# A delta-rule recurrence kept per head: 64x64 state blocks on the quadrants of TensorE

## The chip, the cores and the metric

The kernel runs on one core of one Trainium2 chip. The time is the device time of one execution in microseconds (us); "before" is the median of three runs. A profile of one execution on the same chip goes with it. The engines are named as in the profile: PE is TensorE (matmuls; PEld its weight loads), DVE is VectorE, ACT is ScalarE, POOL is GpSimd, SP is SyncE, which here issues most of the DMAs.

## The reference, cut to what matters

One layer of a hybrid decoder: an input projection, three groups of heads (sparse attention, a recurrence, a memory attention), and an output projection. It is done for a prompt of 1,024 positions and for eight single-position samples. The part that is changed is the recurrence of the prompt, four heads of 64, in float32:

```python
def step(s, inp):
    r_t, k_t, v_t, w_t, kk_t, b_t = inp
    sa = jnp.einsum('bhvk,bhk->bhv', s, -kk_t)
    s = s * w_t[:, :, None, :] + sa[..., None] * b_t[:, :, None, :] + v_t[..., None] * k_t[:, :, None, :]
    return s, jnp.einsum('bhvk,bhk->bhv', s, r_t)
s_fin, ys = lax.scan(step, s0.astype(jnp.float32), xs)
```

Each head has a state of 64x64. The final states are an output of their own.

## The kernel before

**The phases.** Phase 1 projects the prompt through the 28 column blocks of the input weights (`p_pr`: three float32r products for each of eight slices of 128, for the two halves H of the prompt) and runs the recurrence beside it. At its end it makes the keys for attention (`attn_keys`, `prompt_cmp`) and the memory keys (`mem_kv`). Phase 2 is the prompt's attention, phase 3 the samples and the output projection.

**The recurrence in chunks.** The prompt is cut into four quarters Q of 256 positions and each quarter into four chunks n of 64 (n = 2t + p). `rwkv_prep(Q)` makes the inputs, and `rwkv_state(Q)` makes, for each chunk and head, a 64x64 triangular inverse in half-steps of tiny products (`p_iy`, `p_it`), then `p_x`, then four things that the change is about:
- `p_g`: from `W` and the transposed inputs `bkT` and `AM` the transition `PT` of the state (plus the identity, added on DVE) and the read-out `GT`.
- `p_z`: for each chunk the new state, as `bkT x UV` plus `PT x Z`, summed in PSUM; DVE scales it by the decay `gC` and makes `Zn`, which is `Z` of the next chunk. This is the only part that runs one chunk after the other.
- `p_yy`: the output of two chunks, as `GT x Z` plus `AM x UV`.
- `y_c`, the copy of the output by ACT, and `rwkv_out`, its normalisation.

Two heads lie together in one 128x128 state `Z[:, c]`. Only its two diagonal 64x64 blocks hold states; the products fill the off-diagonal blocks too, and `self.blockm` zeroes them when `Zn` is made (L970).

**What sets the order.** `drive(work, fill)` draws the recurrence's steps with priority (`AHEAD`). Each `yield n` of a step is a length in us; `drive` multiplies it by `SLACK` (1.3) and draws that much of the column blocks (`fill`: the first `EARLY` = 17 of the list `cols`) behind it. Before the second quarter's `rwkv_state` stands

```python
while self.open:
    next(fill)
```

which finishes the column block that is open. The remaining blocks, `late`, four of them, come after the fourth quarter, in turn with the making of keys (`bg`). A list scheduler then sets each engine's order by its own estimates, so late blocks can be put between the recurrence's last steps. TensorE's instructions of the fill go through a helper: their line is L87 up to the end of `drive` and for the recurrence, L307 for the late blocks. The pool `pw` holds three PSUM banks, which all tiles of the recurrence share.

Of the kernel before, what the change touches and what calls it, by code (L numbers as in the profile page):

```python
# [114 lines left out]
class Step:  # L115
# [566 lines left out]
    def rwkv_open(self):  # L682
        tc, nc, I = self.tc, self.nc, self.I
        c = self.rc
        cm = self.c_rw = c.tile([128, 480], F32, name="c_rw")
        nc.scalar.dma_start(cm[:], I["c_rw"])
        self.maskA = cm[:, 0:128]
        self.blockm = cm[:, 128:256]
# [23 lines left out]
        self.Z = c.tile([128, 2, 128], F32, name="Z0", tag="Z", bufs=3)  # L712
# [116 lines left out]
    def rwkv_state(self, Q):  # L829
# [103 lines left out]
        GT, PT = [None] * 2, [None] * 2  # L933
        for t in range(2):
# [3 lines left out]
            half = [slice(p * 64, p * 64 + 64) for p in range(2)]  # L938
            for c in range(2):
                for pg, o, p in zip(pgs, half, range(2)):  # L940
                    PE.matmul(pg[:, c * 128:(c + 1) * 128], W[t][o, 2 * c:2 * c + 2, :].rearrange("p a b -> p (a b)"),
                              bkT[t][o, c, p, :], start=True, stop=True)
            for h in range(4):
                for pg, o, p in zip(pgs, half, range(2)):
                    PE.matmul(pg[half[h % 2], 256 + (h // 2) * 64:320 + (h // 2) * 64], W[t][o, h, :],
                              AM[o, 2 * p + t, h, 64:128], start=True, stop=True)
            for p, pg in enumerate(pgs):
                V.tensor_tensor(PT[t][:, :, p, :], pg[:, 0:256].rearrange("p (c e) -> p c e", c=2),
                                bc(I[:, None, :], [128, 2, 128]), op=OP.add)
            for p, pg in enumerate(pgs):  # L950
                V.tensor_tensor(GT[t][:, :, p, :], pg[:, 256:384].rearrange("p (c e) -> p c e", c=2),
                                ar[:, :, t, 1, p, :], op=OP.add)
            yield 1.1
        ys = []
        for t in range(2):
            pyy = self.pw.tile([128, 4, 64], F32, name="p_yy", tag="w")
            Zs = []
            for p in range(2):
                n = 2 * t + p
                Z = self.Z  # L960
                Zs.append(Z)
                pz = self.pw.tile([128, 2, 128], F32, name="p_z", tag="w")
                Zn = self.rc.tile([128, 2, 128], F32, name="Zn", tag="Z", bufs=3)
                for c in range(2):
                    PE.matmul(pz[:, c, :], bkT[t][:, c, p, :], UV[:, n, 2 * c:2 * c + 2, :].rearrange("p a b -> p (a b)"),
                              start=(c == 0), stop=False, skip_group_check=True)
                for c in range(2):
                    PE.matmul(pz[:, c, :], PT[t][:, c, p, :], Z[:, c, :], start=False, stop=(c == 1), skip_group_check=True)
                for c in range(2):
                    V.scalar_tensor_tensor(Zn[:, c, :], pz[:, c, :], self.gC[:, c, n:n + 1], self.blockm,  # L970
                                           op0=OP.mult, op1=OP.mult)
                self.Z = Zn
                if p == 0:
                    yield 0.8
            half = [slice(64 - p * 64, 128 - p * 64) for p in range(2)]
            for c in range(2):
                for p, o in enumerate(half):
                    PE.matmul(pyy[o, 2 * c:2 * c + 2, :].rearrange("p a b -> p (a b)"), GT[t][:, c, p, :], Zs[p][:, c, :],
                              start=(c == 0), stop=False, skip_group_check=True)
            for h in range(4):  # L980
                for p, o in enumerate(half):
                    PE.matmul(pyy[o, h, :], AM[:, 2 * p + t, h, 64:128], UV[:, 2 * t + p, h, :], start=False, stop=(h == 3),
                              skip_group_check=True)
# [29 lines left out]
    def rwkv_close(self):  # L1013
        nc, O = self.nc, self.O
        ps = self.pw.tile([128, 2, 128], F32, name="p_s", tag="w")
        for c in range(2):
            nc.tensor.transpose(ps[:, c, :], self.Z[:, c, :], self.ident[:])
        S = self.rs.tile([128, 2, 128], F32, name="S_out", tag="W0")
        nc.scalar.activation(S[:], ps[:], AF.Copy)
        for h in range(4):  # L1020
            o = slice((h % 2) * 64, (h % 2) * 64 + 64)
            nc.sync.dma_start(O["wkv_prompt"][0, 0, h], S[o, h // 2, o])

# [1377 lines left out]
def host_consts():  # L2401
# [10 lines left out]
    rw = np.zeros((128, 480), np.float32)  # L2412
# [8 lines left out]
    rw[:, 448:480] = s == c  # L2421
    for h in range(2):
# [54 lines left out]
```

## Time and profile before

| what | value |
|---|---|
| median of three runs | 948.95 us (948.5 to 950.33) |
| the profiled execution | 948.73 us, its span 946.9 us |
| PE busy | 911.0 us, 96% of the span |
| DVE busy | 656.6 us, 69% |
| ACT busy | 436.5 us, 46% |
| recurrence, first `p_am` to last `p_yy` | about 93 to 420 us of the span |
| key making and late blocks | about 427 to 500 us |

A matmul's record lasts some 0.2 to 0.4 us from its first row to its last result, and several overlap. So how long a stretch of matmuls occupies PE is read from one start to the next, not from the durations. Each float32 product of the program stands as two instructions in the trace; a float32r product is one.

### The profile page before, as it was taken

How to read it: one execution, taken by the hardware profiler on the slowest of the kernel's cores; microseconds unless marked ns; L12 is line 12 of the kernel's file. 1: busy time of each engine (PE TensorE's matmuls, PEld its weight loads, DVE VectorE, ACT ScalarE, POOL GpSimd, SP SyncE). 2: the span in 40 equal slices, each digit the busy share in tenths (PEclk: the TensorE clock that was granted, in tenths of full speed). 3: DMA queues.
4: the chain of work that ended last, by engine and by line, in shares of the span. 5: the costliest groups of instructions: out<-in, count | busy, mean ns of one | idle time of the engine just before them, and what ended most of it. 6: DMA issues, size and time to landing. Idle time of an engine off the chain costs nothing.

```text
span 946.9 us, 24305 instructions
## 1 busy us (share of the span) xinstructions
PE 911.0 (96%) x9655; PEld 776.5 (82%) x9655; DVE 656.6 (69%) x2029; ACT 436.5 (46%) x979; POOL 179.5 (19%) x270
## 2 busy tenths in 40 slices
PE   8999999999999999999997999999999998999998
PEld 8998888778897888768885888888888887887976
DVE  7668689847693786984447776756678996548454
ACT  7564324233432243213435666566576765324211
POOL 2000000000000000000103444344355675112010
PEclk9999999999999999999999999999999999999999
DMA  8521323131331118216337425140210035976661
GB/s 277 133 68 35 102 58 101 45 81 50 96 94 44 42 61 195 61 57 169 119 101 206 155 69 177 53 143 25 70 41 9 9 113 157 328 248 216 184 233 47
DMA packets 134985, 105.91 MB, mean 112 GB/s; under 512 B 34673, under 2 KB 121272, under 8 KB 134744
## 3 DMA queue, kind: packets, MB, share of 16 engines
q1 hardware_dynamic: 129880, 92.64, 33.4%
q0 software_dynamic: 3200, 10.49, 3.1%
q8 instruction: 76, 1.25, 0.5%
q10 hardware_dynamic: 1792, 1.23, 0.4%
q14 instruction: 37, 0.30, 0.1%
HBM read 85.74 MB, written 22.78 MB: 115 GB/s over the span
## 4 chain that ended last, share of the span: by engine, by line
PE 71%; DVE 16%; ACT 6%; DMA 3%; issue 2%; POOL 1%; SPq 0%; DVEq 0%; ACTq 0%; POOLq 0%
PE p_pr L87 20%; PE p_out L87 9%; PE p_pr L307 7%; PE p_s L87 5%; PE p_pT L87 4%; PE p_o L87 4%; PE p_hid L87 3%; ACT p L1402 3%; DVE p L1401 2%; PE p_z L87 2%; PE p_sc L87 1%; PE p_it L87 1%; PE p_tk L87 1%; DVE pt L1374 1%; PE p_q L87 1%
## 5 line engine op out<-in xcount | busy, mean ns | idle before, releaser
L87 PE MATMUL p_pr<-h,whi 128*128 128x512 f32 (+2 forms) x976 | 238.2, 337 | 0.0
L87 PEld LDWEIGHTS p_pr<-h,whi 128*128 128x128 f32 x976 | 158.7, 190 | 16.9 <-issue 2.6
L87 PE MATMUL p_pr<-h,wlo 128*128 128x512 f32 (+2 forms) x488 | 158.0, 327 | 0.6 <-DVE wlo L284 0.6
L1427 POOL TENSOR_SCALAR p<-p,fac,gates 128x640 f32<-128x640 f32 (+7 forms) x128 | 104.2, 826 | 106.2 <-DVE fac L1424 60.6
L1402 ACT ACTIVATE p<-p,nm 128x640 f32<-128x640 f32 (+7 forms) x128 | 93.0, 728 | 53.1 <-DVE nm L1401 46.6
L87 PEld LDWEIGHTS p_pr<-h,wlo 128*128 128x128 f32 x488 | 92.0, 190 | 9.1 <-DVE wlo L284 0.8
L87 PE MATMUL p_pT<-ident,p 128*128 128x128 f32 x528 | 70.9, 279 | 5.1 <-ACT pt L1372 1.6
L1076 POOL MEMSET w2d<- 128x128 f32 x1 | 0.2, 205 | 398.1 <-PE p_yy L87 398.1
L1401 DVE CUSTOM_DVE_ANT_0 p<-p_s,bmask 128x512 f32<-128x512 f32 (+7 forms) x96 | 60.3, 662 | 18.6 <-PE p_s L87 15.1
L87 PEld LDWEIGHTS p_pT<-ident,p 128*128 128x128 f32 x528 | 57.0, 141 | 16.0 <-issue 6.6
L307 PE MATMUL p_pr<-h,whi 128*128 128x264 f32 (+2 forms) x320 | 68.8, 310 | 0.4 <-ACT whi L283 0.4
L87 PE MATMUL p_o<-pt,vs 128*64 128x128 f32 x1056 | 67.9, 276 | 0.4 <-DVE cat L1460 0.4
L87 PE MATMUL p_s<-kh,qs 128*128 128x512 f32 (+3 forms) x191 | 65.9, 357 | 1.3 <-DVE nm L1401 1.3
L87 PEld LDWEIGHTS p_o<-pt,vs 128*64 128x64 f32 x1056 | 57.0, 137 | 7.2 <-issue 3.8
L283 ACT ACTIVATE whi<-wraw 128x1024 fp32r<-128x1024 f32 x34 | 36.0, 1058 | 57.8 <-PE p_pr L87 47.6
L284 DVE TENSOR_TENSOR wlo<-wraw,whi 128x1024 fp32r<-128x1024 f32 x33 | 40.3, 1222 | 31.4 <-ACT whi L283 31.4
L87 PE MATMUL p_s<-kl,qs 128*128 128x512 f32 (+3 forms) x192 | 60.6, 336 | 0.0
L1374 DVE COPY pt<-p_pT 128x512 f32<-128x512 f32 (+1 forms) x72 | 48.3, 674 | 13.8 <-PE p_pT L87 13.0
L307 PEld LDWEIGHTS p_pr<-h,whi 128*128 128x128 f32 x320 | 51.1, 189 | 3.2 <-ACT whi L283 0.8
L87 PE MATMUL p_out<-woh,chi 128*128 128x512 f32 x128 | 51.7, 404 | 0.0
L87 PE MATMUL p_out<-woh,clo 128*128 128x512 f32 x128 | 50.2, 392 | 0.4 <-DVE clo L2314 0.4
L87 PE MATMUL p_out<-wol,chi 128*128 128x512 f32 x128 | 49.9, 390 | 0.0
(550 smaller groups left out, 1920.9 us busy)
## 6 DMA issues: line engine op xcount, KB each, us to landing
wraw<-in_w_in_dram SPq DMA_DIRECT2D x34, 512.0 KB
pg<-in_c_pool_dram SPq DMA_DIRECT2D x32, 256.0 KB
pg<-in_c_pool_dram SPq DMA_DIRECT2D x48, 128.0 KB
x<-in_x_prompt_dram SPq DMA_DIRECT2D x8, 512.0 KB
z_d<-zt SPq DMA_DIRECT2D x16, 256.0 KB
cat<-z_d SPq DMA_DIRECT2D x8, 512.0 KB
xres<-in_x_prompt_dram POOLq DMA_DIRECT2D x16, 256.0 KB, 3.6
out_dram<-xres POOLq DMA_DIRECT2D x16, 256.0 KB, 3.1
```

Source lines behind the costliest of these rows:

```text
L87: self.last = getattr(self.engine, op)(*a, **k)
L283: nc.scalar.activation(hi[:, :, :n], raw[:, :, :n], AF.Copy)
L284: (low or nc.vector).tensor_tensor(lo[:, :, :n], raw[:, :, :n], hi[:, :, :n].bitcast(F32), op=OP.subtract)
L307: self.last_mm = self.pe.matmul(ps[:m, :b - a], w[:, k, :m], h[k][:, a:b], start=(k == 0 and i == 0), stop=(k == 7 and i == 2))
L1076: nc.gpsimd.memset(w2d[:], 0.0)
L1374: nc.vector.tensor_copy(pt[:, :n], ps[:, :n])
L1401: V.tensor_tensor_reduce(halves(x), halves(ps), m, -1.0, 3.0e38, op0=OP.add, op1=OP.min, accum_out=nm[:, h, b:b + 1])
L1402: A.activation(x, x, AF.Exp, scale=-1.0, bias=nm[:, h, b:b + 1], accum_out=sm[:, h, b:b + 1])
L1427: nc.gpsimd.tensor_scalar(x, x, f[:, h, b:b + 1], gate[:, hd + h, 1 + b:2 + b], op0=OP.mult, op1=OP.mult)
```

## The change

States are kept per head: `Z` is now 128x2x64, with head h of pair c in partitions 64h to 64h+63. `PT` is kept as two 64x64 blocks, and the identity that is added to it is a stacked one (`eye2`, in 64 more columns of the constant `c_rw`). All products of the four tiles are 64 columns wide and use 64 of PE's columns: `p_g` and the state part of `p_yy` and `p_z` use 64 rows and 64 columns (a quadrant), the `UV` parts 128 rows and 64 columns. The `UV` parts are now issued for all four chunks ahead of the chain of states; the chain is four short steps with a yield behind each but the last; the read-out comes at the end for all four chunks. One PSUM bank `p_z` and two `p_yy` banks (one for each head of a pair) serve the whole quarter. `Zn` is one DVE instruction without mask, `y_c` is copied in two pieces of ACT instead of one, and the final transpose writes 64 partitions.

```diff
-        self.blockm = cm[:, 128:256]
+        self.eye2 = cm[:, 480:544]
-        self.Z = c.tile([128, 2, 128], F32, name="Z0", tag="Z", bufs=3)
+        self.Z = c.tile([128, 2, 64], F32, name="Z0", tag="Z", bufs=5)
...
-            PT[t] = self.rs.tile([128, 2, 2, 128], F32, name="PT", tag=f"PT{t}")
-            pgs = [self.pw.tile([128, 384], F32, name="p_g", tag="w") for _ in range(2)]
+            PT[t] = self.rs.tile([128, 2, 2, 64], F32, name="PT", tag=f"PT{t}")
+            pgs = [self.pw.tile([128, 4, 64], F32, name="p_g", tag="w") for _ in range(2)]
+            for k in range(2):
+                for c in range(2):
+                    for h in range(2):
+                        for pg, o, p in zip(pgs, half, range(2)):
+                            x = AM[o, 2 * p + t, 2 * c + h, 64:128] if k else bkT[t][o, c, p, h * 64:h * 64 + 64]
+                            PE.matmul(pg[half[h], 2 * k + c, :], W[t][o, 2 * c + h, :], x, start=True, stop=True)
...
+            if t == 0:
+                yield 0.9
+        pz = self.pw.tile([128, 4, 2, 64], F32, name="p_z", tag="w")
+        for n in range(4):
             for c in range(2):
...
+                for h in range(2):
+                    PE.matmul(pz[half[h], n, c, :], bkT[n // 2][:, c, n % 2, h * 64:h * 64 + 64], UV[:, n, 2 * c + h, :],
+                              start=(n == c == 0), stop=False, skip_group_check=True)
+        yield 0.9
+        pyy = [self.pw.tile([128, 2, 2, 64], F32, name="p_yy", tag="w") for _ in range(2)]
...
+        Zs = [self.Z]
+        for n in range(4):
+            Zn = self.rc.tile([128, 2, 64], F32, name="Zn", tag="Z", bufs=5)
+            for c in range(2):
+                for h in range(2):
+                    PE.matmul(pz[half[h], n, c, :], PT[n // 2][half[h], c, n % 2, :], Zs[n][half[h], c, :],
+                              start=False, stop=True, skip_group_check=True)
+            V.tensor_tensor(Zn[:], pz[:, n], bc(self.gC[:, :, n:n + 1], [128, 2, 64]), op=OP.mult)
+            Zs.append(Zn)
+            if n < 3:
+                yield 0.8
+        self.Z = Zs[4]
+        for t in range(2):
+            for c in range(2):
+                for p, h in ((0, 0), (1, 1), (1, 0), (0, 1)):
+                    PE.matmul(pyy[h][half[1 - p], t, c, :], GT[t][half[h], c, p, :], Zs[2 * t + p][half[h], c, :],
+                              start=False, stop=(c == 1), skip_group_check=True)
...
-            A.activation(y[:], pyy[:], AF.Copy)
+            for h in range(2):
+                A.activation(y[:, h::2], pyy[h][:, t], AF.Copy)
```

The yields of the changed part add to 4.8 where they were 4.4 (both counted from the 0.6 ahead of `p_g`), so `drive` draws more fill in the first quarter. At the second quarter's `while self.open` one more column block is open and is finished there: ahead of that quarter's first `p_g` PE's order has 981 rows of `p_pr` where it had 909, one block of 72 more, and the fill stays that far ahead up to the fourth quarter.

**First quarter, PE.** Before, PE has for the second and third chunk (n = 1, 2; the number before the x is the result's size, the x at the end how many in a row):

```order
L87 MATMUL p_z<-UV,bkT 128x128 x2
L87 MATMUL p_z<-Zn,PT 128x128 x2
L87 MATMUL p_yy<-Z_417,GT 64x128
L87 MATMUL p_yy<-Zn,GT 64x128
L87 MATMUL p_yy<-Z_417,GT 64x128
L87 MATMUL p_yy<-Zn,GT 64x128
L87 MATMUL p_yy<-UV,AM 64x64 x8
L87 MATMUL p_z<-UV,bkT 128x128 x2
L87 MATMUL p_z<-Zn,PT 128x128 x2
```

Now it has, for the first two chunks:

```order
L87 MATMUL p_yy<-UV,AM 64x64 x16
L87 MATMUL p_z<-Z_417,PT 64x64 x4
L87 MATMUL p_tk<-ident,ct 128x128 x4
L87 MATMUL p_pr<-h_0_245,whi 128x264
L87 MATMUL p_pr<-h_0_246,whi 128x264
L87 MATMUL p_pr<-h_0_245,wlo 128x264
L87 MATMUL p_pr<-h_1_247,whi 128x264
L87 MATMUL p_pr<-h_1_248,whi 128x264
L87 MATMUL p_pr<-h_1_247,wlo 128x264
L87 MATMUL p_z<-Zn,PT 64x64 x4
```

The `UV` products stand in one run ahead, and a step of the chain is four products with fill behind it; before, two steps stood next to each other with a read-out between.

**First quarter, DVE.** Before, between the two pairs of `PT` and `GT`:

```order
L398 TENSOR_TENSOR nr_o<-nr_o,nr_sq 128x8x32
L399 TENSOR_TENSOR nr_o<-nr_o,nr_sq 128x8x32
L284 TENSOR_TENSOR wlo<-wraw,whi 128x1024
L948 TENSOR_TENSOR PT<-p_g,ident 128x2x128 x2
L951 TENSOR_TENSOR GT<-p_g,ar 128x2x64 x2
L970 SCALAR_TENSOR_TENSOR Zn<-p_z,gC,c_rw 128x128 x2
```

and now:

```order
L398 TENSOR_TENSOR nr_o<-nr_o,nr_sq 128x8x32
L399 TENSOR_TENSOR nr_o<-nr_o,nr_sq 128x8x32
L946 TENSOR_TENSOR PT<-p_g,c_rw 128x2x64 x2
L948 TENSOR_TENSOR GT<-p_g,ar 128x2x64 x2
L284 TENSOR_TENSOR wlo<-wraw,whi 128x1024
L972 TENSOR_TENSOR Zn<-p_z,gC 128x128
```

The low part of a column block's weights (`wlo`) went behind the second `PT` and `GT`.

**Fourth quarter, PE.** Before, the last chunks stand among the gate block's small products (`p_pr<-h,wraw`), 36 more of which come behind the last `p_yy`, shown here:

```order
L87 MATMUL p_pr<-h_4_254,wraw 32x256
L87 MATMUL p_pr<-h_5_255,wraw 32x256
L87 MATMUL p_pr<-h_5_256,wraw 32x256
L87 MATMUL p_z<-UV,bkT 128x128 x2
L87 MATMUL p_z<-Zn,PT 128x128 x2
L87 MATMUL p_yy<-Zn,GT 64x128 x4
L87 MATMUL p_yy<-UV,AM 64x64 x8
L87 MATMUL p_pr<-h_6_257,wraw 32x256
L87 MATMUL p_pr<-h_6_258,wraw 32x256
```

Now the fill has run out by `p_x`, and the late blocks (L307) stand between the steps:

```order
L87 MATMUL p_g<-bkT,W 64x64 x7
L87 MATMUL p_g<-AM,W 64x64 x8
L87 MATMUL p_z<-UV,bkT 64x64 x16
L87 MATMUL p_yy<-UV,AM 64x64 x16
L87 MATMUL p_z<-Zn,PT 64x64 x4
L307 MATMUL p_pr<-h_5_255,whi 128x256
L307 MATMUL p_pr<-h_5_256,whi 128x256
L307 MATMUL p_pr<-h_5_255,wlo 128x256
L307 MATMUL p_pr<-h_6_257,whi 128x256
L87 MATMUL p_z<-Zn,PT 64x64 x4
```

The whole gate block is moved ahead of the fourth quarter's `p_x`, and 27 rows of the first late block stand ahead of the last `p_yy`. Behind the recurrence, the first transpose of a key tile (`p_k`, L1244) stands behind 102 rows of the four late blocks (288 rows), where it stood behind 52; the last of the eight behind 164, where it stood behind 125; the product that makes the compressed keys (`p_co`) behind 182, where it stood behind 159, and their transpose (`p_k`, L1192) behind 204, where it stood behind 191. From the end of the third late block (216 rows) on, PE has the same order as before.

## Rows read from the trace of the kernel before

**Rows 1.** The page: busy time with its share of the span, and the span in 40 slices (busy tenths of PE, and the granted clock in tenths).

```profile
PE 911.0 (96%) x9655; PEld 776.5 (82%) x9655; DVE 656.6 (69%) x2029; ACT 436.5 (46%) x979; POOL 179.5 (19%) x270
PE   8999999999999999999997999999999998999998
PEclk9999999999999999999999999999999999999999
```

**Rows 2.** Busy time by stretch: from and to in us of the span, its length, then each engine's busy time with its instructions, the granted clock as a share of full speed, DMA share and GB/s.

```profile
100.00:200.00 100.00, 97.97 (x1566) 82.22 (x1563) 78.67 (x254) 33.84 (x72) 0.00 (x0) 0.98 0.24 67
200.00:300.00 100.00, 98.18 (x1186) 82.39 (x1174) 67.28 (x201) 36.65 (x70) 0.00 (x0) 1.00 0.28 78
300.00:400.00 100.00, 95.93 (x1558) 82.64 (x1546) 74.70 (x252) 33.89 (x72) 0.00 (x0) 0.98 0.34 85
400.00:430.00 30.00, 29.84 (x352) 21.65 (x351) 24.06 (x88) 6.95 (x18) 1.92 (x7) 1.00 0.19 57
430.00:480.00 50.00, 48.21 (x350) 41.82 (x349) 22.02 (x62) 20.67 (x44) 2.73 (x5) 1.00 0.48 135
```

**Rows 3.** What PE waited for between 100 and 430 us: total us, times, longest.

```profile
PE p_it L87 <- DVE iY L871: 2.2, 3, 1.3
PE p_it L87 <- DVE Ti L895: 1.9, 2, 1.7
PE p_g L87 <- DVE GT L951: 0.3, 1, 0.3
```

**Rows 4.** The chain of work that ended last, second quarter: start us, length us, what, and how many instructions.

```profile
200.10 0.61 PE p_r L87 x16
...
211.75 1.60 PE p_pr L87 x6
213.35 1.89 PE p_x L87 x32
...
216.14 1.04 PE p_g L87 x24
...
218.77 1.04 PE p_g L87 x24
...
221.40 0.89 PE p_z L87 x8
...
223.69 0.89 PE p_z L87 x8
224.58 1.05 PE p_yy L87 x24
225.63 1.09 PE p_z L87 x8
...
227.41 0.89 PE p_z L87 x8
228.30 1.05 PE p_yy L87 x24
```

**Rows 5.** Instructions of PE in order of time, second quarter: start us, length us, engine, line, result and operands, rows x columns of PE, and the moving operand's partitions x columns.

```profile
206.78 0.75 PE L87 MATMUL p_it<-iT,iY 32*32 32x32 f32 x64
207.47 0.73 PE L87 MATMUL p_pr<-h,whi 128*128 128x512 f32 x2
...
216.72 0.46 PE L87 MATMUL p_g<-AM,W 64*64 64x64 f32 x16
217.11 0.73 PE L87 MATMUL p_pr<-h,whi 128*128 128x512 f32 x2
```

**Rows 6.** The instructions that read `p_g` and `p_z`: count, then ns shortest, median and longest.

```profile
L948 DVE TENSOR_TENSOR PT<-p_g,ident x16: 410/415/425, 133.6 to 410.5; 128x256 f32<-128x256 f32 x16
L951 DVE TENSOR_TENSOR GT<-p_g,ar x16: 277/280/283, 134.2 to 411.0; 128x128 f32<-128x128 f32 x16
L970 DVE SCALAR_TENSOR_TENSOR Zn<-p_z,gC,c_rw x32: 340/343/352, 138.3 to 419.4; 128x128 f32<-128x128 f32 x32
```

**Rows 7.** First quarter, in order of time: PE's first fill behind the second `p_g`, and DVE.

```profile
135.67 0.51 PE L87 MATMUL p_pr<-h,whi 128*128 128x256 f32 x2
...
135.97 1.22 DVE L284 TENSOR_TENSOR wlo<-wraw,whi 128x1024 fp32r<-128x1024 f32 x1
137.11 0.74 DVE L948 TENSOR_TENSOR PT<-p_g,ident 128x256 f32<-128x256 f32 x2
```

**Rows 8.** The chain that ended last, from the end of the recurrence to the last late block: start us, length us, what.

```profile
419.14 1.05 PE p_yy L87 x24
420.19 5.79 PE p_pr L87 x72
425.98 1.17 PE p_tk L87 x10
...
427.75 0.81 PE p_tk L87 x8
428.56 5.60 PE p_pr L307 x46
...
444.23 4.85 DMA kd<-k_d
...
466.37 0.46 PE p_co L1105 x2
...
471.72 0.33 PE p_k L1192
```

More of the change, by code (lines that the diff above doesn't have):

```diff
@@ L684, in rwkv_open @@
         c = self.rc
-        cm = self.c_rw = c.tile([128, 480], F32, name="c_rw")
+        cm = self.c_rw = c.tile([128, 544], F32, name="c_rw")
         nc.scalar.dma_start(cm[:], I["c_rw"])
         self.maskA = cm[:, 0:128]
-        self.blockm = cm[:, 128:256]
+        self.eye2 = cm[:, 480:544]
         self.levels = cm[:, 256:416].rearrange("p (l j) -> p l j", j=32)
@@ L933, in rwkv_state @@
         GT, PT = [None] * 2, [None] * 2
+        half = [slice(p * 64, p * 64 + 64) for p in range(2)]
         for t in range(2):
             GT[t] = self.rs.tile([128, 2, 2, 64], F32, name="GT", tag=f"GT{t}")
-            PT[t] = self.rs.tile([128, 2, 2, 128], F32, name="PT", tag=f"PT{t}")
-            pgs = [self.pw.tile([128, 384], F32, name="p_g", tag="w") for _ in range(2)]
-            half = [slice(p * 64, p * 64 + 64) for p in range(2)]
-            for c in range(2):
-                for pg, o, p in zip(pgs, half, range(2)):
-                    PE.matmul(pg[:, c * 128:(c + 1) * 128], W[t][o, 2 * c:2 * c + 2, :].rearrange("p a b -> p (a b)"),
-                              bkT[t][o, c, p, :], start=True, stop=True)
@@ L943, in rwkv_state @@
[L943 to L952, printed above, removed]
@@ new lines, in rwkv_state @@
+        yield 0.9
[3 more added lines that the diff above has]
+                for h in range(2):
+                    for p in range(2):
+                        PE.matmul(pyy[h][half[1 - p], t, c, :], AM[:, 2 * p + t, 2 * c + h, 64:128], UV[:, 2 * t + p, 2 * c + h, :],
+                                  start=(t == c == 0), stop=False, skip_group_check=True)
+        Zs = [self.Z]
[9 more added lines that the diff above has]
+                yield 0.8
@@ L954, in rwkv_state @@
+        self.Z = Zs[4]
+        for t in range(2):
+            for c in range(2):
+                for p, h in ((0, 0), (1, 1), (1, 0), (0, 1)):
+                    PE.matmul(pyy[h][half[1 - p], t, c, :], GT[t][half[h], c, p, :], Zs[2 * t + p][half[h], c, :],
+                              start=False, stop=(c == 1), skip_group_check=True)
         ys = []
         for t in range(2):
[L956 to L983, printed above, removed]
@@ L984, in rwkv_state @@
             y = self.rs.tile([128, 4, 64], F32, name="y_c", tag=f"y_c{t}")
-            A.activation(y[:], pyy[:], AF.Copy)
+            for h in range(2):
+                A.activation(y[:, h::2], pyy[h][:, t], AF.Copy)
             ys.append(y)
@@ L1016, in rwkv_close @@
         for c in range(2):
-            nc.tensor.transpose(ps[:, c, :], self.Z[:, c, :], self.ident[:])
-        S = self.rs.tile([128, 2, 128], F32, name="S_out", tag="W0")
-        nc.scalar.activation(S[:], ps[:], AF.Copy)
+            nc.tensor.transpose(ps[:64, c, :], self.Z[:, c, :], self.ident[:])
+        S = self.rs.tile([64, 2, 128], F32, name="S_out", tag="W0")
+        nc.scalar.activation(S[:], ps[:64], AF.Copy)
         for h in range(4):
-            o = slice((h % 2) * 64, (h % 2) * 64 + 64)
-            nc.sync.dma_start(O["wkv_prompt"][0, 0, h], S[o, h // 2, o])
+            nc.sync.dma_start(O["wkv_prompt"][0, 0, h], S[:, h // 2, (h % 2) * 64:(h % 2) * 64 + 64])
     def load_w1(self, tiles):
@@ L2411, in host_consts @@
     mat = np.eye(128, dtype=np.float32)
-    rw = np.zeros((128, 480), np.float32)
+    rw = np.zeros((128, 544), np.float32)
     s, c = p[:, None] % 64, np.arange(128)[None, :]
@@ L2421, in host_consts @@
     rw[:, 448:480] = s == c
+    rw[:, 480:544] = p[:, None] % 64 == np.arange(64)
     for h in range(2):
```

5 lines of the change are left out of this document (4 added, 1 removed).

## The prediction

> **What bounds the kernel now.** I read the page first. PE is busy for 96% of the span, in nearly every slice, with the granted clock at its upper level of 2.4 GHz [rows 1]. The changed work ends at 420 us, so I looked at stretches next: from 100 to 430 us PE is idle for 2.0, 1.8, 4.1 and 0.2 us, 8.1 us in all, and in the 50 us behind it for 1.8 us [rows 2]. DVE is the next engine, with 67 to 79% up to 400 us [rows 2]. The waits name where PE's idle time is: in the inverse's half-steps, on DVE's `iY` and `Ti` (4.1 us in five waits), and 0.3 us on `GT` [rows 3]. No row names `Zn`: the chain of states costs PE no wait, because fill lies between its steps. So PE's own time is the bound here. What the change takes from PE is won, unless a new wait takes it, and what it takes from DVE or ACT is not.
>
> **What one quarter costs now.** In the second quarter the pieces of the chain give `p_g` 1.04 and 1.04, `p_z` 0.89, 0.89, 1.09 and 0.89, `p_yy` 1.05 twice: 7.94 us [rows 4]. Four quarters are about 31.8 us.
>
> **What it costs after.** `p_z` shows the stream: eight instructions of 128 columns on the whole array in 0.89 us, 0.111 us each [rows 4], so 0.056 for 64 columns. No row has the new shapes in the new order, but three pieces show how neighbours run side by side.
> - `p_x`: 32 instructions of 128 columns on two quadrants take 1.89 us [rows 4]. Two at a time they would stream for 32 x 0.111 / 2 = 1.78; 0.11 is left.
> - `p_r`: 16 of 64 columns on two quadrants take 0.61 us [rows 4]; 16 x 0.056 / 2 = 0.45; 0.16 is left.
> - `p_g<-AM,W`: 16 of 64 columns on four quadrants, from 216.72 to 217.11, 0.39 us [rows 5]; 16 x 0.056 / 4 = 0.22; 0.17 is left.
>
> So they do overlap, two or four at a time, and each visit to a smaller shape costs some 0.11 to 0.17 us. I take 0.15.
>
> Streams per quarter after, two instructions to a product: `p_g` 64 over four quadrants 0.89; the `UV` parts of `p_z` 32 over two halves 0.89; the state steps 32 over two quadrants 0.89; `AM` x `UV` 32 over two halves 0.89; `GT` x `Z` 32 over four 0.44; together 4.0 us. Visits: six groups with fill between, and two changes of row count inside groups, 8 x 0.15 = 1.2. That is 5.2 us, a saving of 2.74 a quarter, 11.0 in all: the upper end. The lower end comes from whole-piece means: 0.39/16 = 0.024 us on four quadrants for 96 instructions, and 0.61/16 = 0.038 on two for 96, 6.0 us, a saving of 1.9, 7.8 in all. The short state steps (eight instructions) pay a visit each and are nearest to `p_r`, the long runs to `p_x`; I take 2.3 a quarter, **9.2 us**. One price speaks against these rates. `p_it` has 64 instructions on 32x32 tiles from 206.78 to 207.47, 0.011 us each [rows 5], so no floor above that holds for one instruction among tiles. The Trainium skill (TensorEngine Tiling (Array Packing), section Instruction Overhead) says that each matmul has about 60 cycles of overhead and warns against cutting a dimension that is already small. By that, as an estimate, 192 instructions of 25 ns and the visits are 6.0 us a quarter, and the term would be 7.8; the row of `p_it` doesn't agree.
>
> **Other engines.** `Zn` is one instruction for two; the nearest row is `GT`, of the same size from PSUM, 0.28 us, so 16 x 0.28 for 32 x 0.34, and `PT` shrinks from 0.415 to the same 0.28 [rows 6]. DVE gives up 6.4 + 2.2 = 8.6 us. That is off the path; at most it shortens the waits on `iY` and `Ti`, 0 to 1.5 us, and I count 0. ACT's two smaller copies of `y_c`, the wider constant and the memset lie beside PE work that has nothing to do with them: 0.
>
> **The new chain of states.** A step now needs its products (8 x 0.056 / 2 + 0.15 = 0.37 us) and DVE's 0.28. In the first three quarters 3 to 12 rows of fill lie between, over 0.7 us, and the chain has no row among the waits even now [rows 3], with 0.68 us of DVE a step. 0.
>
> **The fourth quarter.** The fill is a whole block ahead, so the half-steps of the inverse have the gate block's small products between them, and the last steps late blocks of 3 to 8 rows. The 36 gate products behind the old end (13,440 columns together) took 5.79 us [rows 8]; eight of 264 columns, the cover that some half-steps get now, are 0.9 us, where six rows of fill gave 1.60 [rows 4]. Today five waits there average 0.8 us [rows 3]. I expect two or three more of these, **+2.0 us** (bounds: 0.3, if DVE is as quick as in the other half-steps, and 4).
>
> **The tail.** Work is moved, not added: ahead of the last `p_yy` now lie the gate block (5.79), its transposes (1.17 and 0.81) and 27 rows of a late block (5.60/46 = 0.122 each, 3.3) [rows 8], 11.1 us that came behind it. So that `p_yy` ends at 420.2 + 11.1 - 9.2 + 2.0 = 424.1, 3.9 us later, with 11.1 us less PE work behind it. What then waits for the end of the recurrence (`y_d`, the keys' DMAs and pools) starts later and has fewer late rows to hide it. From `p_co` to the compressed keys' `p_k` 5.35 us pass [rows 8]; 32 late rows stood there (159 to 191 in the order) and 22 stand there now (182 to 204), some 4.5 us of work with a transpose beside them: 0.8 of wait. The key tiles come in pairs through DMAs of up to 4.85 us [rows 8]; with 62 late rows between the first and last `p_k` in place of 73 I give them 1. Those two make 1.8, less the share of today's 1.8 us of idle time that lies in the same places [rows 2]: **+1.5 us** (bounds 0 and 6). From the end of the third late block on the order is the old one, and the gain is carried to the end: phase 2 starts behind `mem_kv`, which these blocks' weights and matmuls pace.
>
> **Sum.** -9.2 + 2.0 + 1.5 = -5.7 us on the profiled execution's 948.73, 943.0. The median of the runs is 0.2 us above that execution, so I predict **943.2 us**.
>
> **Rivals.** A change of 0.2% (1.9 us) is about what a measurement of this kernel can tell from none.
> - *The tail eats the gain.* If the tail is a chain of latencies, its idle time grows by 5 to 7 us: 947 to 949, no change. For it: everything there starts 3.9 us later. Against it: PE is busy for 48.2 of the 50 us behind 430 [rows 2], so it is work and not waiting that sets its length. If it were latency alone, the time would be 948.7 + 3.9 = 952.6; for that the idle time would have to grow by 11.1.
> - *Slower: the three banks of `pw`.* `p_z` and the two `p_yy` now fill the pool, so PE's `AM` x `UV` run must wait until DVE has read the second pair of `p_g`. In the first quarter DVE came to it 1.4 us after PE was done, behind a `wlo` of 1.22 us [rows 7], and PE did not care. If PE now waits that and a second `wlo`, 2.7 us in each quarter, the sum is -5.7 + 10.8 = +5.1: 954. It decides from 1.4 us of wait a quarter, where nothing measurable is left. Against it: `PT` and `GT` now stand ahead of that `wlo`, and `p_z`'s `UV` run (1 us) and 12 rows of fill (1.4 us) lie between. The Trainium skill (the same page, PSUM Bottleneck) warns of this: tiling speeds up TensorE but not the reading of PSUM.
> - *No overlap.* If 64-wide products ran one after another, 192 x 0.056 = 10.7 us a quarter, 2.8 more than now even without the visits: with 2.0 and 1.5, 963. `p_r` and `p_g<-AM,W` speak against it [rows 4, 5].
> - *More than forecast.* The upper end of the tiles, and DVE's relief shortening the inverse's waits: -11.0 - 1.5 + 1.5 + 0.5 = -10.5: 938.
>
> **Chances.** The forecast, with a gain of 3.5 to 8.5 us, 0.62; more, 0.08; a gain of 1.9 to 3.5, where waits take most, 0.09; the tail rival 0.12; slower by the banks or by a tail of latencies alone 0.08; no overlap 0.01. The forecast's own range is 940 to 945.5. Eight in ten lie in **939.5 to 948.2**, which leaves out half of the tail rival, the slower ones and the upper end. Faster by over 0.2%: 0.79; within: 0.12; slower: 0.09.
>
> **What the profile after would show.** `p_g` pieces of 0.6 us, state steps of about 0.4, and 5.2 to 6.0 us a quarter in place of 7.9: the first term. PE waits on `iY` and `Ti` up by 2 us around the gate block: the second. The last `p_yy` ending near 424, the third late block's end 5 to 6 us earlier than before: the third. A wait of PE on `GT` of over 1 us in each quarter would be the banks; a wait on `kd` or on POOL's copies of several us the tail. I am wrong if quadrants work slower in this order than in the three pieces that I have, or if the late start of the keys costs more than PE's rows show.

## The result, and the profile after

The changed kernel takes **942.38 us** (median of seven runs, 936.75 to 945.56) where the kernel before took 948.95 beside it (seven runs, 948.35 to 951.69): the medians are 6.6 us or 0.7% apart, and the ratio estimated from all runs is 0.9913, with a 95% interval of 0.9884 to 0.9942. The forecast was 943.2 us, with a range of 939.5 to 948.2. The profiled execution took 943.56 us, its span 941.8.

The page after, busy time and slices, beside [rows 1]:

```profile
PE 904.4 (96%) x9911; PEld 768.2 (82%) x9911; DVE 645.6 (69%) x2013; ACT 435.4 (46%) x987; POOL 178.7 (19%) x270
PE   8999999999999999999897999999999998999997
PEclk9999999999999999999998999999999999999999
```

PE is busy for 6.6 us less, with 256 instructions more, and the span is only 5.1 shorter: PE's idle time grew by 1.5. One slice of the granted clock, the 22nd, shows an 8.

The stretches that [rows 2] shows of before (from:to, length, busy time with instructions of PE, PEld, DVE, ACT, POOL, granted clock, DMA share, GB/s):

```profile
100.00:200.00 100.00, 99.78 (x1466) 84.81 (x1468) 79.00 (x261) 34.16 (x76) 0.00 (x0) 1.00 0.28 78
200.00:300.00 100.00, 97.78 (x1279) 79.77 (x1270) 65.86 (x201) 38.03 (x73) 0.00 (x0) 1.00 0.24 68
300.00:400.00 100.00, 95.90 (x1721) 80.06 (x1720) 73.78 (x256) 33.06 (x72) 0.00 (x0) 0.97 0.36 93
400.00:430.00 30.00, 29.46 (x508) 22.91 (x509) 15.91 (x67) 6.28 (x20) 1.98 (x7) 1.00 0.22 61
430.00:480.00 50.00, 46.39 (x324) 38.91 (x323) 25.23 (x67) 23.20 (x46) 2.67 (x5) 1.00 0.47 134
```

PE's idle time from 100 to 430 us is 0.2 + 2.2 + 4.1 + 0.5 = 7.1 us (8.1 before), and in the 50 us behind it 3.6 (1.8 before).

The second quarter in the chain that ended last (start us, length us, what, instructions), beside [rows 4]:

```profile
223.18 0.62 PE p_g L87 x32
...
225.40 0.62 PE p_g L87 x32
226.03 1.08 PE p_z L87 x32
...
228.70 1.08 PE p_yy L87 x32
229.79 0.38 PE p_z L87 x8
...
234.69 0.47 PE p_yy L87 x26
```

The two `p_g` take 0.62 us each (1.04 before), the `UV` run of `p_z` and the `AM` run of `p_yy` 1.08 each, the first three steps 0.38 each (the rows left out, at 231.06 and 233.04, are like the one at 229.79), and the last step with the read-out 0.85 (from 234.31 to the end of the last row). That is 5.39 us; it was 7.94.

Where the gain goes is seen when the span is cut at two points that stand in the same place of PE's order in both kernels: the end of the memory keys' products (`p_mo`), and the start of the transposes that wait for `pcq`, at the start of phase 2. Before (same columns as above):

```profile
0.00:499.85 499.85, 485.08 (x5823) 417.35 (x5824) 347.67 (x1112) 197.31 (x398) 11.45 (x39) 0.99 0.33 94
499.85:521.05 21.20, 15.38 (x86) 11.48 (x85) 18.72 (x69) 11.76 (x29) 7.42 (x8) 1.00 0.79 233
521.05:946.00 424.95, 410.50 (x3748) 347.71 (x3748) 290.16 (x849) 227.37 (x553) 160.61 (x224) 1.00 0.40 127
```

And after:

```profile
0.00:492.25 492.25, 476.33 (x6079) 406.86 (x6080) 336.40 (x1096) 196.21 (x406) 11.32 (x39) 0.99 0.34 96
492.25:514.23 21.98, 16.38 (x86) 12.37 (x85) 18.70 (x69) 11.77 (x28) 7.43 (x8) 0.91 0.76 228
514.23:941.00 426.77, 411.69 (x3748) 348.96 (x3748) 290.54 (x849) 227.42 (x553) 159.92 (x224) 0.99 0.40 126
```

Phase 1 ends 7.6 us earlier: 8.75 us less of busy time, 1.15 more of idle time. The start of phase 2, with the same 86 instructions of PE, takes 0.8 us more at a granted clock of 0.91; PE's idle time in it is 5.6 us, where it was 5.8. From there to the end of the span it is 427.6 us after and 425.85 before, 1.7 more, again with the same instructions of PE. So of 7.6 us won, 2.5 were given back where nothing was changed.

What happens there, PE from 499 to 515 us after (start, length, instruction; in brackets the idle time before it and what ended it):

```profile
502.02 0.33 PE L87 MATMUL p_s<-kh,qs 128*128 128x128 f32 x1 [2.47 <-DVE nm L1401]
...
514.23 1.08 PE L87 MATMUL p_pT<-ident,pcq 128*128 128x128 f32 x4 [2.38 <-DVE pcq L1349]
```

And the stretch behind the second of these waits:

```profile
513.00:514.00 1.00, 0.00 (x0) 0.00 (x0) 1.00 (x1) 0.18 (x2) 1.00 (x2) 0.76 0.99 334
514.00:515.00 1.00, 0.77 (x5) 0.80 (x5) 0.96 (x4) 0.00 (x0) 1.00 (x1) 0.50 0.86 292
...
520.00:521.00 1.00, 1.00 (x6) 0.77 (x5) 0.46 (x4) 0.09 (x1) 0.79 (x1) 0.82 0.49 138
```

The granted clock is 0.50, the lower level of 1.2 GHz, from 513.5 us, still within the wait, to 520.4 us (0.76 and 0.82 are means over slices in which it changes). In the same way it is at that level from 503.3 to 506.7, behind the first wait. At half clock 7 us do the work of 3.5. The kernel before has one such stretch there, of 3.4 us from 520.9 us on, at its wait for `pcq`. Each stretch in the profiles lasts 3.4 us or a multiple of it; at half clock that is, as an estimate, 1.7 us of work lost, or a multiple.

### The profile page after: what moved, and what is told of

The parts are those of the page before. It is cut to its first block, busy times and chain, and to the rows that moved or that the text cites. A ratio compares the mean times of both kernels' runs of the same rounds, so it can differ in the third digit from the quotient of the medians.

```text
span 941.8 us, 24822 instructions
## 1 busy us (share of the span) xinstructions
PE 904.4 (96%) x9911; PEld 768.2 (82%) x9911; DVE 645.6 (69%) x2013; ACT 435.4 (46%) x987; POOL 178.7 (19%) x270
## 3 DMA queue, kind: packets, MB, share of 16 engines
q8 instruction: 78, 1.28, 0.6%
q10 hardware_dynamic: 1792, 1.26, 0.4%
## 4 chain that ended last, share of the span: by engine, by line
PE 71%; DVE 17%; ACT 5%; DMA 3%; issue 2%; SPq 1%; POOL 0%; DVEq 0%; ACTq 0%; POOLq 0%
PE p_pr L87 20%; PE p_out L87 9%; PE p_s L87 5%; PE p_pT L87 5%; PE p_pr L307 4%; PE p_o L87 4%; PE p_hid L87 3%; ACT p L1402 2%; DVE p L1401 2%; DMA kd<-k_d 1%; PE p_iy L87 1%; PE p_it L87 1%; PE p_sc L87 1%; PE p_mo L1155 1%; PE p_tk L87 1%
## 5 line engine op out<-in xcount | busy, mean ns | idle before, releaser
L307 PE MATMUL p_pr<-h,whi 128*128 128x264 f32 (+2 forms) x320 | 69.4, 310 | 0.0
L307 PEld LDWEIGHTS p_pr<-h,whi 128*128 128x128 f32 x320 | 51.5, 188 | 3.1 <-issue 0.2
```

Of the source, the lines that this page charges most:

```text
L307: self.last_mm = self.pe.matmul(ps[:m, :b - a], w[:, k, :m], h[k][:, a:b], start=(k == 0 and i == 0), stop=(k == 7 and i == 2))
```

## The experiments

The theory at this point was: the gain is TensorE's time in the tiles, and it needs neighbours on different quadrants; part of it is lost to half-clock stretches behind PE's waits, which also spread the runs over 9 us. The rivals: the gain is the new order; the moved fill is what costs; the spread has nothing to do with the clock. Each set of kernels ran beside the kernel before on the same chip.

**The changed kernel again (again, again2).** No edit.

> The changed kernel once more. Its seven runs lay between 936.8 and 945.6 us, a spread of 9 us where the kernel before has 3, and the profiled one (943.6) loses some 2.5 us at the start of phase 2, where the granted clock falls to 0.5 twice behind waits of PE of 2.5 and 2.4 us. Theory: the spread comes from such falls of the clock, which differ from run to run; then the median is 940 to 944 again, the spread over 5 us, and a profile that lies lower or higher by some us shows fewer or more half-clock slices, 0.5 us for each us at half clock. Rival: the spread was of the first set alone, and the runs lie within 3.5 us of each other now, around 942.

> The changed kernel once more, beside the next three on the same chip. So far its runs are ordered by the granted clock of the whole run: 944.7 to 943.6 us at 0.989, 943.6 to 942.3 at 0.991, 938.5 at 0.995. Theory (each half-clock stretch costs 1.7 us, and how many a run has differs): median 941 to 944, and a run at a clock of 0.996 or more lies near 938. Rival: the spread has another cause, and time and clock go apart.

Measured: 942.96 us (six runs, 938.45 to 944.7; ratio 0.9941, 0.9917 to 0.9964) and 942.76 (six runs, 937.5 to 945.77; 0.9929, 0.9903 to 0.9956). The spread stayed, and within each of these two sets it follows the clock. In again2 the runs, by their mean granted clock, are 0.987: 942.64 and 945.77; 0.988: 942.89; 0.989: 943.01; 0.991: 940.95; 0.996: 937.5. The kernel before does the same: its 23 runs beside after_warm go from 946.6 at 0.998 to 955.1 and 954.4 at 0.987 and 0.985. At an equal clock the two kernels are further apart than their medians: at 0.991 the six runs of before have a median of 951.2 and the four of the changed kernel 942.3; at 0.996 twelve runs have 947.6 and three 938.9. That is 8.7 to 8.9 us. But the 19 runs of the changed kernel have a mean clock of 0.991 and the 51 of before in these sets 0.994; 0.0026 of 945 us are 2.5 us, an estimate of what the lower clock takes and about the difference to the measured 6 us. The relation is looser in the first set, where one run took 936.75 us at 0.994 and another 942.6 at 0.996. The changed kernel's first profile holds five half-clock stretches of 3.4 us, those of again and again2 five and six, that of before three.

**The fill where it was (same_fill).**

```diff
             if t == 0:
-                yield 0.9
+                yield 0.7
...
-        yield 0.9
+        yield 0.7
         pyy = [self.pw.tile(...
```

> The changed kernel with two yields of 0.7 in place of 0.9, so that they add to 4.4 as before the change. No column block is drawn ahead: 909 rows of fill lie ahead of the second quarter's products, and the last read-out comes behind 36 gate products fewer and 27 late rows fewer, all as before the change. It parts the tiles from the moved fill. Theory A (the moved fill costs the tail 1.8 us of idle time and phase 2 a late start): last p_yy near 410, the idle time between the recurrence's end and phase 2 back at some 2 us, time 1 to 3 us below the changed kernel, 939.5 to 941.5. Theory B (the moved work gave cover to the inverse's half-steps, whose idle time fell by 1 us, and the tail's cost is small): the idle time of 100 to 430 us back at 8, time within 1 us of the changed kernel or up to 1 us above it.

Measured: 941.9 us (937.75 to 944.3; ratio 0.9926, 0.99 to 0.9953), not to be told from the changed kernel. What PE waited for from 430 to 530 us (total us, times, longest):

```profile
PE p_s L84 <- DVE zt L319: 1.6, 1, 1.6
PE p_s L87 <- DVE nm L1401: 1.1, 3, 0.5
PE p_k L1244 <- DMA kd<-k_d: 0.8, 1, 0.8
```

The same view of the changed kernel:

```profile
PE p_k L1244 <- DMA kd<-k_d: 2.9, 3, 2.0
PE p_s L87 <- DVE nm L1401: 2.7, 2, 2.5
PE p_pT L87 <- DVE pcq L1349: 2.4, 1, 2.4
```

Both theories have their part: the waits for the key tiles' DMAs fall from 2.9 to 0.8 us, and the idle time from 100 to 430 us is back at 8.1. The two nearly cancel, as theory B had it; the moved fill decides nothing that this measurement shows.

**The tiles in the old order (tiles_old_order).**

```diff
-        pz = self.pw.tile([128, 4, 2, 64], ...)   # UV parts of all chunks, then four steps, then read-out
+            yield 1.1
+        for t in range(2):
+            for p in range(2):
+                pz = self.pw.tile([128, 2, 64], F32, name="p_z", tag="w")
+                ... # UV parts and PT x Z of one chunk, Zn
+                if p == 0:
+                    yield 0.8
+            pyy = [self.pw.tile([128, 2, 64], F32, name="p_yy", tag="w") for _ in range(2)]
+            ... # GT x Z and AM x UV of two chunks, y_c
```

> The 64x64 blocks of the changed kernel in the order of the kernel before: for each pair of chunks two steps, each with its own p_z bank and its UV products just ahead, and the read-out behind each pair; the old yields too. It parts the tiles from the new chain. Theory (the gain is TensorE's time in the tiles): a quarter takes some 5.4 us plus a few visits more (two groups more a quarter, 0.15 each), 5.7 in place of 7.9, and the time is 939 to 943, with the fill where it was before. Rival (the gain is the order: the UV products ahead, the fill behind each step): the steps of 0.4 us now stand next to each other with no fill, PE waits for Zn and for the read of the p_z bank between them, 0.3 to 0.7 us twelve times, and the time is 945 to 949.

Measured: 941.09 us (937.63 to 942.48; ratio 0.9924, 0.9902 to 0.9945). The second quarter in its chain, from the second `p_g` to the read-out of the first two chunks:

```profile
217.30 0.76 PE p_z L87 x16
...
219.65 0.58 PE p_z L87 x10
...
220.41 0.85 PE p_yy L87 x26
```

With the two `p_g` (0.62 each) and a second pair like this the quarter is 5.83 us. The steps stand next to each other and PE waits for `Zn` in none of them: in these groups, between 100 and 430 us, it waited once for `y_c`, 0.3 us, and once for `GT`, 0.2 us. So the gain is the tiles, and the new order of the chain, whose quarter is 0.44 us shorter, is worth nothing that this measurement shows in the time.

**Neighbours on the same tile (no_turn).**

```diff
-            for c in range(2):
-                for h in range(2):
+            for h in range(2):
+                for c in range(2):
```

in the state steps, and in the same manner in the other groups: `p_g` in runs of four instructions on one quadrant, `GT` x `Z` in runs of eight, the `UV` part of `p_z` and `AM` x `UV` in runs of 16 on one half.

> The changed kernel with its products in another order within each group, so that neighbours go to the same rows and columns of TensorE as long as possible (all of one quadrant or half, then all of the next), nothing else. Theory (the products run side by side because neighbours lie on different quadrants): p_g 1.8 us in place of 0.62, p_z UV and p_yy AM 1.8 in place of 1.08, a quarter near 9.5 to 10.8 in place of 5.4, the time 958 to 963. Rival (TensorE takes 64-column products at this rate in any order): no change, 942 within 2 us.

Measured: 950.95 us (twelve runs, 947.84 to 955.18; ratio 1.003, 1.0012 to 1.0047): slower than before the change, 8 us above the changed kernel. Its chain in the second quarter:

```profile
224.84 0.69 PE p_g L87 x30
...
227.79 1.83 PE p_z L87 x32
...
231.22 1.83 PE p_yy L87 x32
233.04 0.39 PE p_z L87 x8
...
237.97 1.11 PE p_yy L87 x29
```

Runs of 16 on one half go one after another: 32 instructions of 64 columns in 1.83 us are 0.057 each, the whole stream rate, against 1.08 when the halves alternate. Runs of eight take 1.11 where alternation takes 0.47. Runs of four cost little: `p_g` 0.69 against 0.62, a state step 0.39 against 0.38. So the theory is right in kind, and its 9.5 to 10.8 us a quarter was too much by the groups that have short runs; the quarter is 7.7 us, 2.3 more than with alternation, and four of them make 9.2 us, beside the 8 us measured. The Trainium skill (TensorE: Matmul & The Clock Gate, section The mechanism) says that weight loads are pulled ahead of running matmuls within a window of 64 instructions, while the matmuls themselves keep their order. The trace agrees with the kept order: runs of 16 on one half did not overlap with the next half's runs (1.83 us for 32), though 16 is well within 64.

**Work in the waits (after_warm, before_warm, w2_9).** A helper issues n products of the identity with itself into a bank that nothing reads, ahead of the waiting instructions; this is the edit of w2_9:

```diff
+    def keep_warm(self, n):
+        ps = self.pO.tile([128, 128], F32, name="p_w", tag="o")
+        for _ in range(n):
+            self.te._do("matmul", ps[:], self.ident[:], self.ident[:], start=True, stop=True)
...
+        if tag == "c" and 7 not in self.pcT:
+            self.keep_warm(9)
```

> The changed kernel, and at the start of phase 2 ten products of the identity with itself (128x128, float32, into a bank that nothing reads) ahead of the scores that wait 2.5 us for nm and ten more ahead of the transposes that wait 2.4 us for pcq; ten take 2.2 us, so they fit into the waits and are work that the result doesn't need. Theory (half-clock stretches come behind idle time of PE): no slice of 495 to 522 us is below 0.97, where the two profiles of the changed kernel lost 5.1 us each there, and the time is 2 to 5 us below the changed kernel's, 938 to 941. Rival 1 (the clock falls for another reason, such as the products just behind): half-clock slices there as before, time 942 to 944. Rival 2: the products are late and push the rows behind them, 943 to 946.

Measured: 945.82 us (twelve runs, 944.14 to 948.62; ratio 0.9964, 0.9947 to 0.9982), 3 us slower than the changed kernel, as rival 2 had it in time but not in cause. Its profile around the place:

```profile
497.14 2.48 PE L87 MATMUL p_w<-ident 128*128 128x128 f32 x20
499.66 0.33 PE L87 MATMUL p_s<-kh,qs 128*128 128x128 f32 x1
...
505.22 0.55 PE L87 MATMUL p_s<-kh,qs 128*128 128x512 f32 x1 [3.47 <-DVE nm L1408]
```

The products fit into the wait and delayed nothing by themselves. But the list scheduler counts them, and with them it gave DVE another order: the subtraction and the sum of `pcq` now stand ahead of the next scores' minimum `nm`, and PE waits 3.5 us for that. A half-clock stretch of 3.4 us stands at that longer wait (505.5 to 509 us), and none behind the second group of products. So the time of this run says nothing on the clock; it shows what a moved order of DVE costs.

> The kernel before with the ten products ahead of the transposes that wait for pcq alone, its one wait of over 2 us. In its profile that wait was followed by a half-clock stretch of 3.4 us, which cost 1.7. Theory: that stretch is gone, time 0.5 to 1.7 us below the kernel before, 947 to 948.2. Rival: no change, since the clock falls there anyway.

Measured: 947.44 us (twelve runs, 945.25 to 950.72; ratio 0.998, 0.9961 to 0.9999). In its profile the transposes come at 520.6 us with no half-clock slice behind them. But the profile, of one of the slowest runs (950.41 us), holds five stretches elsewhere, where that of before holds three. The size, 1.7 us or 0.2%, is what was expected, but the interval reaches almost to 1.

> The changed kernel with nine products of the identity (2.0 us, work that the result doesn't need) ahead of the transposes that wait 2.4 us for pcq. The products in front of the other wait, tried in the run after_warm, moved instructions on DVE, ACT, POOL and SP as well; these nine leave the order of every engine's other instructions as it is. Theory (the clock falls behind an idle PE): no half-clock slice within 5 us behind that wait, in a place where both profiles of the changed kernel had one (one of them two), and a median 1 to 2.5 us below the changed kernel's. Rival: a half-clock stretch there all the same, no difference.

Here the other instructions keep their order, in the trace too. The time in which the changed kernel's clock fell, as w2_9's profile has it:

```profile
513.00:514.00 1.00, 0.83 (x7) 0.87 (x8) 0.96 (x4) 0.17 (x1) 1.00 (x1) 1.00 0.91 328
514.00:515.00 1.00, 1.00 (x9) 0.86 (x9) 0.90 (x5) 0.47 (x2) 0.09 (x1) 1.00 0.93 290
```

The products fill the wait (0.17 us of it is left) and the clock stays at the upper level, where all three profiles of the changed kernel have a half-clock stretch of 3.4 to 7 us. The other profiles bear this out: in all eight without products in that place (before, after, again, again2, same_fill, tiles_old_order, no_turn, nry2) a half-clock stretch begins in the wait for `pcq` or within 1.5 us behind it, and in none of the six with products does one begin there. In this place, then, keeping PE busy kept the clock. The time did not follow: 942.82 us (940.83 to 944.44; ratio 0.9941, 0.9922 to 0.996), beside 942.76 of again2, and the runs' clocks are 0.987 to 0.994. In its profile stretches stand behind other waits, of 1.28 us at 321, of 2.2 at 501 and of 1.0 at 790. Which waits have one differs from run to run: the wait of 1.0 us at 790 to 794 has one in the profiles of again and w2_9 and none in those of the changed kernel and again2, though the wait is the same.

**A second buffer (nry2, nry2_w2_6).** DVE ahead of the 2.5 us wait in the changed kernel:

```profile
499.94 0.42 DVE L383 TENSOR_TENSOR nr_y<-p_mo,rq_r 128x256 f32<-128x256 f32 x1 [1.78 <-DMA out_dram<-nr_y]
...
500.74 1.21 DVE L1401 CUSTOM_DVE_ANT_0 p<-p_s,bmask 128x1024 f32<-128x1024 f32 x1
```

`nr_y` has one buffer; its second use waits until the first has left by DMA, and the minimum `nm` for PE's next scores stands behind it on DVE.

```diff
-        y = self.tk.tile([128, n, 64], F32, name="nr_y", tag=f"nry{cols}", bufs=nb)[:parts]
+        y = self.tk.tile([128, n, 64], F32, name="nr_y", tag=f"nry{cols}", bufs=2 if cols == 256 else nb)[:parts]
```

> The changed kernel with two buffers in place of one for the normalised memory keys nr_y. In its profile DVE waits 1.8 us at 498.1 until the first half's nr_y has left by DMA, and the scores' minimum nm, for which PE waits 2.5 us, stands behind that on DVE. Theory: DVE's wait is gone, PE's wait for nm falls from 2.5 to 0.7 us or less, and the time by 1.7 us, and by 1.7 more where the clock no longer falls behind it: 939 to 941.5. Rival: the wait for pcq behind it grows by as much, since it goes by DVE and ACT and not by PE, and the time stays at 942 to 943.

Measured: 940.37 us (939.63 to 943.35; ratio 0.991, 0.9887 to 0.9933). PE's waits from 430 to 530 us:

```profile
PE p_pT L87 <- POOL p L1427: 2.5, 2, 1.6
PE p_pT L87 <- DVE pcq L1349: 1.6, 1, 1.6
PE p_s L87 <- DVE nm L1401: 0.8, 3, 0.5
```

The wait of 2.5 us for `nm` fell to 0.5 as expected, and the one for `pcq` shrank by 0.8 us; but the waits for `p`, which POOL scales, ahead of its transposes grew from 0.5 to 2.5 us. Its profile has the transposes for `pcq` at 511.2 us, 3.0 earlier than the changed kernel's. At a granted clock of 0.991 its four runs lie at 939.6 to 940.6 us, and the four of the changed kernel at 941.0 to 943.6. But the buffer is not all that changed: the list scheduler also moved instructions on DVE (the first minima `nm` and the making of `pcq`), on ACT, POOL and SP. The run shows what the second buffer brings together with these orders; how much is the buffer's wait alone stays open.

> Two buffers for nr_y, as in the run nry2, and six products of the identity (1.3 us) ahead of the transposes that waited 1.6 us for pcq there; all other instructions stand as in nry2, which had 940.4 us. Theory: the half-clock stretch behind that wait, which nry2's profile has, is gone; 938 to 940. Rival: 940.4 within 1 us, since another stretch takes its place.

Measured: 940.1 us (934.47 to 940.42; ratio 0.9896, 0.9873 to 0.9919), no gain over nry2 that can be told. No half-clock slice stands behind the wait for `pcq`; in its profile others stand at 321, 382, 505, 669 and 792 us. The rival was right. The one at 669 us stands behind no wait:

```profile
668.00:669.00 1.00, 1.00 (x12) 0.98 (x11) 0.97 (x4) 0.16 (x1) 0.00 (x0) 1.00 0.00 0
...
670.00:671.00 1.00, 1.00 (x11) 0.88 (x11) 0.37 (x4) 0.21 (x1) 0.00 (x0) 0.50 1.04 311
```

PE is busy for 9.98 of the 10 us from 658 to 668. The profiles of nry2, fill_nry2_w2_6, old_order_warm and before_warm have such a stretch too, at 669 to 679 us behind a PE that was as busy. So waits are not the only place where the clock falls, and what sets off these falls stays open.

**Together (old_order_warm, fill_nry2_w2_6).**

> The 64x64 blocks in the old order, with seven products of the identity ahead of phase 2's first scores, which wait 1.6 us for zt, and ten ahead of the transposes that wait 2.4 us for pcq. In the profile without them the clock is at half from 496 to 507 and from 513 to 517 us, 6.8 us lost. Theory: these stretches are gone; such stretches differ from run to run, so the median falls by less than that, 2 to 5 us, from 941.1 to 936 to 939, some 11 us below the kernel before. Rival: the time is that of the blocks in the old order, 940 to 942.

Measured: 940.36 us (938.1 to 947.2; ratio 0.9902, 0.9875 to 0.9929), which the rival had (940 to 942). Its products, too, moved instructions on DVE and the queues. Four of its six runs lie at 938.1 to 941.9 and a clock of 0.995 or 0.996; the profiled one, 947.2, has 0.987 and a half-clock stretch from 508 to 519 us.

> All that seemed to help, together: the changed kernel with yields that add to 4.4 (the fill where it was before the change), two buffers for nr_y and the six products ahead of the wait for pcq. If the parts add up (0.5 to 1 for the fill, 2 for nr_y, 1 to 1.7 for the products) it takes 937.5 to 939.5, some 10 us less than the kernel before. Rival: the gains lie within one another, and it takes 940 to 941 like each of them.

Measured: **939.05 us** (936.48 to 940.37; ratio 0.9894, 0.9876 to 0.9913), the lowest median of all, 9.7 us below the kernel before and some 3.7 below the changed kernel in the same set (0.9929, 0.9903 to 0.9956; the intervals overlap). It lies in the range of the theory; against nry2 and nry2_w2_6 it is not shown to be faster.

## Why the prediction came out right, step by step

**The tiles, -9.2 us: right.** The pieces give -2.55 a quarter, -10.2 in all; PE's busy time up to the end of the memory keys fell by 8.75, with two half-clock stretches in that part of both profiles. The forecast lies between the two readings, and both lie within its bounds of 7.8 and 11.0; the difference of 8.7 to 8.9 us at an equal clock agrees. `p_g` was to take 0.6 and takes 0.62, a step 0.37 and takes 0.38, the quarter 5.2 to 6.0 and is 5.39. The rate was read from three pieces that all alternate between tiles; no_turn shows that this was a condition and not only a circumstance, and that without it the change would have made the kernel slower. The rival without overlap was thus nearer than its 0.01 said: it hangs on how the loops of five groups are nested.

**DVE, 0.28 us an instruction: right**, as the rows that answer [rows 6] show (count; ns shortest, median, longest):

```profile
L946 DVE TENSOR_TENSOR PT<-p_g,c_rw x16: 277/281/294, 133.6 to 415.8; 128x128 f32<-128x128 f32 x16
L972 DVE TENSOR_TENSOR Zn<-p_z,gC x16: 280/290/292, 139.3 to 421.3; 128x128 f32<-128x128 f32 x16
```

DVE is busy for 11 us less, and nothing of it is seen in PE's idle time where the fill stands as before: same_fill has 8.1 us from 100 to 430 us, as the kernel before. **The banks:** PE waited 0.2 us for `GT` in all, so that rival is out.

**The fourth quarter's waits, +2.0: too high.** From 300 to 430 us PE's idle time is 4.6 us where it was 4.2 [rows 2], +0.4, near the lower bound of 0.3. The waits from 100 to 430 us (the view of [rows 3]; the one on `zt` stands at 275 us):

```profile
PE p_pr L87 <- DVE zt L319: 2.0, 1, 2.0
PE p_iy L87 <- DVE rq_t L135: 1.9, 1, 1.9
PE p_it L87 <- DVE Ti L895: 1.5, 2, 1.3
```

The five half-step waits are not joined by more; those on `iY` are gone (the longest, 1.3 us, stood at 380 us), and a wait of 1.9 us on `rq_t` stands at 384 us in their place. From 100 to 300 us, where the forecast counted nothing, the idle time fell from 3.85 to 2.4 us. That goes with the block that was drawn ahead: in same_fill, without it, the idle time there is 4.2 us. The step that failed is the price of "two or three more of these at 0.8".

**The tail, +1.5: right**, 3.6 us of idle time for 1.8, and in the place that was named: the key tiles' DMAs, 2.9 us where it was 1.0. Its rows in the chain:

```profile
421.19 0.52 PE p_yy L87 x26
...
449.66 0.63 PE p_k L1244 x4
...
480.00 0.49 PE p_pr L307 x4
```

The last `p_yy` ends at 421.7 and not at 424.1, by the larger saving and the waits that did not come. The third late block's end, in front of the row at 480.00, is 7.4 us earlier than in the chain of before, where that row stands at 487.35, and not 5 to 6. As a mechanism the tail rival fell: key making takes longer, but by less than the work that moved.

**"The gain is carried to the end": wrong.** By the end of phase 1 the gain was 7.6 us, 1.9 more than the forecast's sum; 2.5 of it were lost in phase 2, whose order on PE is unchanged. The forecast had no term for the clock, although rows of before carry it: 0.98 in two stretches of [rows 2]; in the same trace PE waits 2.4 us for `pcq`, with a half-clock stretch at the end of that wait. The first 0.8 us are lost ahead of the `pcq` transposes: the scores came 9.4 us earlier than before (495.58 for 504.99), DVE's `nm` only 7.1, because it stands behind a DMA out of one buffer (a wait of 1.78 us, 1.26 before). PE's wait of 2.5 us for `nm` takes the place of one of 1.65 for `zt`, so its idle time did not grow there. The other 1.7 us, behind these transposes, are what one half-clock stretch more would cost, and the profile has one more; that it is the cause is argued and not shown, since w2_9 took the stretch at the `pcq` wait away and the median stayed. So a median within 1 us of the forecast is in part luck: it comes from two misses of some 2 us with opposite signs.

What stays open is why the changed kernel's runs have a lower clock, 0.991 against 0.994 on the mean. Its waits of over 1 us are no more in number than before (six to seven of PE between 100 and 530 us in both profiles), those at the start of phase 2 are longer (2.5 and 2.4 for 1.65 and 2.4). nry2, which has no wait of over 2 us there, ran at 0.990 all the same, so the length of these waits doesn't settle it, and neither do waits alone: five profiles have a half-clock stretch behind a busy PE.

## What to carry to other kernels

Products that use half the rows or columns of TensorE run side by side only if near neighbours in the order go to different quadrants or halves; the innermost loop should run over the tiles, and here that alone was worth 8 us. When PE is the bound and a change takes work from it, follow the gain past the changed part: the next wait behind DVE or a DMA takes a piece, and a half-clock stretch may take 1.7 us more. Where runs spread by 1%, put the granted clock beside each run's time before explaining a difference of 2 or 3 us, and where a scheduler sets the orders, compare them on every engine before a kernel with added work is called an experiment on that work alone.

## What the runs showed of the hardware

- Interleaved on quadrants, 32 float32 instructions of 64 columns take 0.62 us, 0.019 each; on halves 1.08, 0.034 each; one tile after another 0.057 each. Alternating every four instructions is nearly as good as every two (0.69 and 0.62), every eight is not (1.11 for the 0.47 of alternation).
- In most cases the granted clock falls to 1.2 GHz in or behind waits of PE of 1.0 to 3.5 us, for 3.4 us at a time, sometimes twice in a row although PE is fully busy again (513 to 520 us above). The same wait has such a stretch in one run and none in another, and the wait of 2.0 us at 449.66 in the changed kernel's profile had none (1.00 from 430 to 480). In five profiles it also falls at 669 to 679 us behind 10 us in which PE was busy throughout.
- A run's time goes with its mean granted clock, with some scatter: in the changed kernel 938.5 us at 0.995 and 944.7 at 0.989, in the kernel before 946.6 at 0.998 and 955.1 at 0.987.
